# Gate and up products of two feed-forward layers: weights stationary, 256 token columns moving

## The chip, the core and the metric

The kernel runs on one core of one Trainium2 chip. The time is the device time of one execution in microseconds (us). Before the change three runs gave 2736.33, 2738.47 and 2739.03 us; their median is 2738.47. The profile is of one further execution.

## The reference

Two transformer blocks follow each other on 256 tokens of width 2048, all in float32. The first has a gated linear recurrence and sliding-window attention, the second gated linear attention; each ends in a SwiGLU feed-forward layer with a hidden width of 5632. Only these two layers are touched by the change:

```python
# first block: h2 is the normed x, scaled and shifted per channel
h2 = modulate(rms_norm(x, norm2_g[l]), sh2, sc2)
gate, up = jnp.split(h2 @ w_ffn_in[l], 2, axis=-1)
x = x + g2 * ((jax.nn.silu(gate) * up) @ w_ffn_out[l])
...
# second block
g, u = jnp.split(h @ w_gu, 2, axis=-1)
x = x + (jax.nn.silu(g) * u) @ w_down        # h = rms_norm(x) * gain
```

## The kernel before

Activations lie channel-major: 128 channels on the partitions, 256 tokens along the free axis. A group of 512 channels is one tile of 128x4x256 (a slot; there are 24).

**Weights.** Every weight matrix is streamed once, in chunks of 512 inputs x 512 outputs, 1 MB each. `split` loads a chunk into one of three `raw` buffers through SP's queue, and then works on halves (128x1024): ScalarE writes the rounded part `hi` (L173), VectorE the rest `lo` = raw - hi (L175). There are three `hi` and three `lo` buffers of half a chunk. A product of two numbers is made of three matmuls: hi x hi, hi x lo and lo x hi, so activations are kept as hi/lo pairs as well (`Pair`; `split_act` makes one, L225 and L226). A `tc.high_priority` block lets the scheduler put the loads and splits of weights ahead of other work.

**The two forms of `accumulate`.** In the plain form a block of 128x128 weights is the stationary operand and 256 token columns of the activation pair move (L197, L199, L201): 48 matmuls a chunk, whose result is channel-major. With `tokens=True` 128 tokens of the activation are stationary and 512 weight columns move (L190 to L192): 24 matmuls a chunk, whose result is token-major (128 tokens x 512 channels).

**The feed-forward layers.** `swiglu` is called twice, first with `gate1`, `up1`, `update1`, later with `gate2`, `up2`, `update2`. It takes the 11 groups of hidden channels in two parts, of 6 and of 5. For each group j `gate(j)` makes 4 chunks of the gate product (PSUM tiles `fgps`) and `up(sg, j)` 4 chunks of the up product (`fups`); then the down product (`fops`) runs over the groups of this part. So each layer has 88 chunks of gate and up and 44 of down.

Gate and up use `tokens=True`. What they leave in `sg` is token-major, but the down product needs channel-major. `turned` makes that: two `pump` steps after `up`, four 128x128 transposes on TensorE for each half group (L666, PSUM tile `tps`), then L668 and L669 write the hi and lo parts of `hid` straight from PSUM. A token's norm factor is then one number per partition; `by_token` (L336 on) turns the factor row into that column with two transposes. In layer 1's first group the norm's shift has to be added after the product, and it is a row of 512 (`fb`), which `matvec(..., row=True)` makes with one matmul that has ones as its stationary operand (L255).

**Order of work.** The kernel is plain Python that a scheduler orders per engine. `project` calls `pump` between chunks, which advances spawned generators (such as `second_norm`) and, by a credit, one step of a matrix-vector product (`ada_steps`: a load into one of five `mvw` buffers and one VectorE instruction, L247). In layer 1, two such strips of 16 steps run beside gate and up. `mvw` and `raw` loads share SP's queue there. Each engine runs its instructions in order.

Of the kernel before, what the change touches and what calls it, by code (L numbers as in the profile page):

```python
# [18 lines left out]
P = 128  # L19
# [30 lines left out]
def block_pair_kernel(ctx: ExitStack, tc: tile.TileContext, a: dict):  # L50
# [41 lines left out]
    def halves(t):  # L92
        return [t[:, 0:2, :], t[:, 2:4, :]]
# [85 lines left out]
    def accumulate(ps, ap, src, first, last, tokens=False):  # L179

        parts = split(ap, tokens)
        for kk in range(4):
            hi, lo = parts[kk // 2]
            wk = kk % 2
            fst, lst = first and kk == 0, last and kk == 3
            if tokens:
                for t in range(2):
                    tsl = slice(t * P, (t + 1) * P)
                    xh, xl = src.hi(kk)[:, tsl], src.lo(kk)[:, tsl]
                    nc.tensor.matmul(ps[t], xh, hi[:, wk, :], start=fst, stop=False)  # L190
                    nc.tensor.matmul(ps[t], xh, lo[:, wk, :], start=False, stop=False)  # L191
                    nc.tensor.matmul(ps[t], xl, hi[:, wk, :], start=False, stop=lst)  # L192
                continue
            for f in range(4):
                wsl = slice(f * P, (f + 1) * P)
                o = ps[f // 2][:, f % 2, :]
                nc.tensor.matmul(o, hi[:, wk, wsl], src.hi(kk), start=fst and f % 2 == 0,  # L197
                                 stop=False, skip_group_check=True)
                nc.tensor.matmul(o, hi[:, wk, wsl], src.lo(kk), start=False, stop=False,  # L199
                                 skip_group_check=True)  # L200
                nc.tensor.matmul(o, lo[:, wk, wsl], src.hi(kk), start=False, stop=lst,  # L201
                                 skip_group_check=True)

    def banks(name, tokens=False):
        return [bank(name, [P, 512] if tokens else [P, 2, T]) for _ in range(2)]
# [25 lines left out]
    nc.scalar.activation(cact, v("c", 0, 16), AF.Silu)  # L231
    mod = const.tile([P, 96], F32, name="mod")

    def matvec(srcs, col, width, done, queue=nc.gpsimd, row=False):


        state = {}

        def step(k):
            def run():  # L240
                w = mvw.tile([P, width], F32, tag="mvw", name="mvw")
                queue.dma_start(w, srcs[k])
                if k == 0:
                    state["acc"] = slot("mva", shape=[P, width])
                    nc.vector.tensor_scalar(state["acc"], w, col(0), None, ALU.mult)
                else:
                    nc.vector.scalar_tensor_tensor(state["acc"], w, col(k), state["acc"],  # L247
                                                   ALU.mult, ALU.add)
            return run

        def reduce():
            n = width // P
            ps = bank("mvp")
            if row:
                nc.tensor.matmul(ps[:, 0:width], ones, state["acc"], start=True, stop=True)  # L255
                done(ps[:, 0:width])
                return
            for f in range(n):
                nc.tensor.matmul(ps[:, f:f + 1], state["acc"][:, f * P:(f + 1) * P],
                                 ones[:, 0:1], start=True, stop=True)  # L260
            done(ps[:, 0:n])

        return [step(k) for k in range(NK)] + [reduce]
# [81 lines left out]
    def pair(ap):  # L345
        return ap.unsqueeze(1).to_broadcast([P, 2, T])
# [282 lines left out]
    while steps:  # L629
# [7 lines left out]
    steps += matvec([a["w_ffn_in"][0, k // 4][:, k % 4, :] for k in range(NK)],  # L637
                    lambda k: shift2[:, k:k + 1], 512, lambda ps: nc.vector.tensor_copy(fb, ps), nc.sync,
                    True)
    credit[0], credit[1] = 0.0, 1.3  # L640
    ssq = SumSq("ss2")
    gx = []
# [11 lines left out]
        steps.pop(0)()  # L654


    def turned(sv):

        p = Pair("hid")
        yield p  # L660
        for b in range(2):
            tp = bank("tps", [P, 2, T])
            for i in range(2):
                f = 2 * b + i
                for t in range(2):
                    nc.tensor.transpose(tp[:, i, t * P:(t + 1) * P], sv[:, t, f * P:(f + 1) * P],  # L666
                                        ident)
            nc.scalar.activation(p.his(b), tp, AF.Copy)  # L668
            nc.vector.tensor_tensor(p.los(b), tp, f32(p.his(b)), ALU.subtract)  # L669

    def swiglu(w_in, w_out, gate, up, update):
        for n, half in enumerate((range(0, 6), range(6, FG))):
            hid, turns = [], []
            for j in half:
                sg = gate(j)
                pump()
                gen = turned(up(sg, j))
                hid.append(next(gen))
                turns.append(spawn(gen, 2))
                pump()  # L680
            for f in range(NG):
                chunks = chunks_of(w_out, f, list(half))
                ps = banks("fops")
                for c in range(len(chunks)):
                    finish(turns[c])
                    accumulate(ps, chunks[c], hid[c], c == 0, c == len(chunks) - 1)
                    if c < len(chunks) - 1:
                        pump()
                update(n, f, ps)
                pump()  # L690

    h2 = [None] * NG
# [12 lines left out]
    norm_task = spawn(second_norm())  # L705

    def gate1(j):
        sg = slot("sg", shape=[P, 2, 512])
        ps = project(chunks_of("w_ffn_in", j), gx if j == 0 else h2, "fgps", True)
        if j == 0:  # L710
            finish(norm_task)
            for t in range(2):
                nc.vector.scalar_tensor_tensor(sg[:, t, :], ps[t], norm2["invp"][:, t:t + 1],
                                               fb, ALU.mult, ALU.add)
            nc.scalar.activation(sg, sg, AF.Silu)
        else:
            for t in range(2):
                nc.scalar.activation(sg[:, t, :], ps[t], AF.Silu)
        return sg

    def up1(sg, j):
        ps = project(chunks_of("w_ffn_in", FG + j), h2, "fups", True)
        for t in range(2):
            nc.vector.tensor_tensor(sg[:, t, :], ps[t], sg[:, t, :], ALU.mult)
        return sg

    steps += ada_steps(10, nc.sync) + ada_steps(11, nc.sync)
    credit[0], credit[1] = -6.0, 0.9
# [220 lines left out]
    norm5 = {}  # L949

    def last_norm():
        inv = inv_rms(ssq.mean(onesd), "inv5")
        yield 1
        norm5["inv"] = by_token(inv, "invp5")

    norm_task = spawn(last_norm(), 2)

    def gate2(j):
        sg = slot("sg", shape=[P, 2, 512])
        ps = project(chunks_of("ffn_w_gu", j), h2, "fgps", True)  # L960
        finish(norm_task)
        for t in range(2):
            nc.scalar.activation(sg[:, t, :], ps[t], AF.Silu, scale=norm5["inv"][:, t:t + 1])
        return sg

    def up2(sg, j):
        ps = project(chunks_of("ffn_w_gu", FG + j), h2, "fups", True)
        for t in range(2):
            nc.vector.scalar_tensor_tensor(sg[:, t, :], ps[t], norm5["inv"][:, t:t + 1],
                                           sg[:, t, :], ALU.mult, ALU.mult)  # L970
        return sg

    def update2(n, f, ps):
        for b, part in enumerate(halves(x[f])):
# [99 lines left out]
```

## Time and profile before

| | |
|---|---|
| median of three runs | 2738.47 us (2736.33 to 2739.03) |
| the profiled execution, its own time | 2733.5 us |
| span of that execution | 2731.7 us |
| granted TensorE clock | 0.999 |
| 512-column matmuls of gate and up | 4224 (L190 to L192, three groups each of `fgps` and `fups`) |
| first matmul of layer 1's gate to layer 1's end | about 856 to 1589 us |
| layer 2 | from about 1998 us to the end |

How to read the quoted lines. A page of the profile gives, by engine, busy time, share of the span and number of instructions. A row of groups gives line, engine, operation, out<-in by the program's names, shapes, count, busy time, the mean ns of one, and the idle time before it with what ended it. A row of waits gives who waited for whom, the total in us, how often, and the longest. A row of the timeline gives start (us), length (us), engine, line and operation, with a count where equal ones are merged, and in brackets the idle time before. A matmul's length contains its passage through the array, so the pace is read from the distance between starts.

### The profile page before, as it was taken

The numbers are of one execution on the slowest core, as the hardware profiler recorded it, in microseconds if no ns is written. First come the engines' busy times: TensorE is split into PE (matmuls) and PEld (weight loads), VectorE is DVE, ScalarE is ACT, GpSimd is POOL, SyncE is SP. The second block draws the span as 40 slices with busy tenths as digits, with TensorE's granted clock in tenths as the row PEclk, the third lists the DMA queues.
The fourth block names the chain that finished last, engine by engine and source line by source line (L and its number), as shares of the span: only waits on it lengthen the run. The fifth ranks groups of instructions, "written<-read, shape, count | busy, mean of one in ns | idle before, by whom it ended". The sixth has DMA issues, their size and how long they took to land.

```text
span 2731.7 us, 43911 instructions
## 1 busy us (share of the span) xinstructions
PE 2680.5 (98%) x18612; PEld 2479.3 (91%) x18612; DVE 1782.3 (65%) x2000; ACT 1310.7 (48%) x1525; POOL 25.7 (1%) x52
## 2 busy tenths in 40 slices
PE   4999999999999999999999999999999999999999
PEld 3999999999999888999888999899988889988899
DVE  8887876888887865444545667866654544444544
ACT  3446637864445444434444545655544444344443
POOL 1100000000000000000000000000000000000000
PEclk9999999999999999999999999999999999999999
DMA  9984696769875866555555544444555555555554
GB/s 351 370 311 147 221 341 226 273 243 351 336 278 194 311 238 217 186 200 187 191 192 185 195 170 170 142 152 171 200 186 187 195 188 188 199 186 194 190 195 161
DMA packets 100166, 602.00 MB, mean 220 GB/s; under 512 B 11121, under 2 KB 11633, under 8 KB 40577
## 3 DMA queue, kind: packets, MB, share of 16 engines
q1 hardware_dynamic: 93056, 574.03, 59.1%
q0 software_dynamic: 6912, 25.17, 2.3%
q8 instruction: 145, 2.38, 0.3%
q14 instruction: 53, 0.43, 0.0%
HBM read 597.06 MB, written 2.10 MB: 219 GB/s over the span
## 4 chain that ended last, share of the span: by engine, by line
PE 95%; DVE 2%; issue 1%; DMA 1%; ACT 1%; SPq 0%; DVEq 0%; ACTq 0%
PE fgps L192 6%; PE fgps L191 6%; PE fgps L190 6%; PE fops L197 6%; PE fups L190 6%; PE fups L192 6%; PE fups L191 6%; PE fops L201 6%; PE fops L199 6%; PE part L197 2%; PE part L199 2%; PE part L201 2%; PE lops L201 1%; PE ups L197 1%; PE wops L197 1%; PE ups L201 1%
## 5 line engine op out<-in xcount | busy, mean ns | idle before, releaser
L175 DVE TENSOR_TENSOR lo<-raw,hi 128x1024 fp32r<-128x1024 f32 x928 | 1134.3, 1224 | 842.9 <-ACT hi L173 841.2
L173 ACT ACTIVATE hi<-raw 128x1024 fp32r<-128x1024 f32 x928 | 983.1, 1060 | 1270.4 <-PE fups L192 274.5
L197 PE MATMUL fops<-hid,hi 128*128 128x256 f32 x1408 | 389.0, 276 | 0.0
L201 PE MATMUL fops<-hid,lo 128*128 128x256 f32 x1408 | 388.7, 276 | 0.0
L199 PE MATMUL fops<-hid,hi 128*128 128x256 f32 x1408 | 388.6, 276 | 0.0
L190 PE MATMUL fups<-hi,h 128*128 128x512 f32 x704 | 274.0, 389 | 0.0
L192 PE MATMUL fups<-hi,h 128*128 128x512 f32 x704 | 273.9, 389 | 0.0
L191 PE MATMUL fups<-lo,h 128*128 128x512 f32 x704 | 273.9, 389 | 0.0
L199 PEld LDWEIGHTS fops<-hid,hi 128*128 128x128 f32 x1408 | 264.3, 188 | 0.1
L197 PEld LDWEIGHTS fops<-hid,hi 128*128 128x128 f32 x1408 | 264.3, 188 | 0.2
L201 PEld LDWEIGHTS fops<-hid,lo 128*128 128x128 f32 x1408 | 264.3, 188 | 0.0
L190 PE MATMUL fgps<-hi,h 128*128 128x512 f32 x672 | 263.5, 392 | 0.0
L192 PE MATMUL fgps<-hi,h 128*128 128x512 f32 x672 | 261.8, 390 | 0.0
L191 PE MATMUL fgps<-lo,h 128*128 128x512 f32 x672 | 261.6, 389 | 0.0
L247 DVE SCALAR_TENSOR_TENSOR mva<-mvw,cact,mva 128x1024 f32<-128x1024 f32 x180 | 230.6, 1281 | 26.6 <-DMA mvw<-ada_w 24.5
L191 PEld LDWEIGHTS fups<-lo,h 128*128 128x128 f32 x704 | 132.2, 188 | 27.4
L190 PEld LDWEIGHTS fups<-hi,h 128*128 128x128 f32 x704 | 132.2, 188 | 27.4
L192 PEld LDWEIGHTS fups<-hi,h 128*128 128x128 f32 x704 | 132.2, 188 | 27.4
L192 PEld LDWEIGHTS fgps<-hi,h 128*128 128x128 f32 x672 | 126.1, 188 | 26.2
L190 PEld LDWEIGHTS fgps<-hi,h 128*128 128x128 f32 x672 | 126.2, 188 | 25.6
L191 PEld LDWEIGHTS fgps<-lo,h 128*128 128x128 f32 x672 | 126.2, 188 | 25.5
L197 PE MATMUL part<-h,hi 128*128 128x256 f32 x512 | 145.2, 284 | 0.0
(322 smaller groups left out, 5410.7 us busy)
## 6 DMA issues: line engine op xcount, KB each, us to landing
raw<-w_in SPq DMA_DIRECT2D x88, 1024.0 KB, 5.7
raw<-w_ffn_in SPq DMA_DIRECT2D x88, 1024.0 KB, 4.9
raw<-ffn_w_gu SPq DMA_DIRECT2D x88, 1024.0 KB, 4.8
mvw<-ada_w SPq DMA_DIRECT2D x144, 512.0 KB, 7.0
raw<-gla_w_in SPq DMA_DIRECT2D x48, 1024.0 KB, 4.9
raw<-w_ffn_out SPq DMA_DIRECT2D x44, 1024.0 KB, 4.8
raw<-ffn_w_down SPq DMA_DIRECT2D x44, 1024.0 KB, 4.9
mvw<-ada_w POOLq DMA_DIRECT2D x48, 512.0 KB, 8.5
```

The costliest lines, as they stand in the source:

```text
L173: nc.scalar.activation(hi, rb, AF.Copy)
L175: nc.vector.tensor_tensor(lo, rb, f32(hi), ALU.subtract)
L190: nc.tensor.matmul(ps[t], xh, hi[:, wk, :], start=fst, stop=False)
L191: nc.tensor.matmul(ps[t], xh, lo[:, wk, :], start=False, stop=False)
L192: nc.tensor.matmul(ps[t], xl, hi[:, wk, :], start=False, stop=lst)
L197: nc.tensor.matmul(o, hi[:, wk, wsl], src.hi(kk), start=fst and f % 2 == 0, stop=False, skip_group_check=True)
L199: nc.tensor.matmul(o, hi[:, wk, wsl], src.lo(kk), start=False, stop=False, skip_group_check=True)
L201: nc.tensor.matmul(o, lo[:, wk, wsl], src.hi(kk), start=False, stop=lst, skip_group_check=True)
L247: nc.vector.scalar_tensor_tensor(state["acc"], w, col(k), state["acc"], ALU.mult, ALU.add)
```

## The change

Gate and up now use the plain form, as the rest of the kernel does. Their result is channel-major, so `turned` goes, and `split_act` makes `hid` right behind the product. The norm factor multiplies as a row broadcast over partitions (`pair(inv)`), so both `by_token` calls of these layers go. In layer 1's first group VectorE multiplies by the factor and ScalarE adds the shift as a bias, from an `fb` of 128x4. In layer 2 ScalarE could take the factor as a scale before; now VectorE multiplies the gate product by it, ScalarE takes Silu of the whole group into a new tile `sv`, and VectorE multiplies that by the factor again, which stands for the factor on the up product.

```diff
-    fb = slot("fb", shape=[P, 512])
+    fb = slot("fb", shape=[P, 4])
...
-                gen = turned(up(sg, j))
-                hid.append(next(gen))
-                turns.append(spawn(gen, 2))
+                hid.append(up(sg, j))
                 pump()
             for f in range(NG):
-                chunks = chunks_of(w_out, f, list(half))
...
-                    finish(turns[c])
-                    accumulate(ps, chunks[c], hid[c], c == 0, c == len(chunks) - 1)
...
+                update(n, f, project(chunks_of(w_out, f, list(half)), hid, "fops"))
...
-        norm2["invp"] = by_token(norm2["inv"], "invp2")
...
     def gate1(j):
-        sg = slot("sg", shape=[P, 2, 512])
-        ps = project(chunks_of("w_ffn_in", j), gx if j == 0 else h2, "fgps", True)
+        sg = slot("sg")
+        ps = project(chunks_of("w_ffn_in", j), gx if j == 0 else h2, "fgps")
         if j == 0:
             finish(norm_task)
-            for t in range(2):
-                nc.vector.scalar_tensor_tensor(sg[:, t, :], ps[t], norm2["invp"][:, t:t + 1],
-                                               fb, ALU.mult, ALU.add)
-            nc.scalar.activation(sg, sg, AF.Silu)
+            for b, part in enumerate(halves(sg)):
+                nc.vector.tensor_tensor(part, ps[b], pair(norm2["inv"]), ALU.mult)
+            for f in range(4):
+                nc.scalar.activation(sg[:, f, :], sg[:, f, :], AF.Silu, bias=fb[:, f:f + 1])
...
     def up1(sg, j):
-        ps = project(chunks_of("w_ffn_in", FG + j), h2, "fups", True)
-        for t in range(2):
-            nc.vector.tensor_tensor(sg[:, t, :], ps[t], sg[:, t, :], ALU.mult)
-        return sg
+        ps = project(chunks_of("w_ffn_in", FG + j), h2, "fups")
+        for b, part in enumerate(halves(sg)):
+            nc.vector.tensor_tensor(part, ps[b], part, ALU.mult)
+        return split_act(sg, "hid")
...
     def gate2(j):
-        sg = slot("sg", shape=[P, 2, 512])
-        ps = project(chunks_of("ffn_w_gu", j), h2, "fgps", True)
+        sg = slot("sg")
+        ps = project(chunks_of("ffn_w_gu", j), h2, "fgps")
         finish(norm_task)
-        for t in range(2):
-            nc.scalar.activation(sg[:, t, :], ps[t], AF.Silu, scale=norm5["inv"][:, t:t + 1])
-        return sg
+        for b, part in enumerate(halves(sg)):
+            nc.vector.tensor_tensor(part, ps[b], norm5["inv"], ALU.mult)
+        sv = slot("sv")
+        nc.scalar.activation(sv, sg, AF.Silu)
+        for b, part in enumerate(halves(sv)):
+            nc.vector.tensor_tensor(part, part, norm5["inv"], ALU.mult)
+        return sv
 
     def up2(sg, j):
-        ps = project(chunks_of("ffn_w_gu", FG + j), h2, "fups", True)
-        for t in range(2):
-            nc.vector.scalar_tensor_tensor(sg[:, t, :], ps[t], norm5["inv"][:, t:t + 1],
-                                           sg[:, t, :], ALU.mult, ALU.mult)
-        return sg
+        ps = project(chunks_of("ffn_w_gu", FG + j), h2, "fups")
+        for b, part in enumerate(halves(sg)):
+            nc.vector.tensor_tensor(part, ps[b], part, ALU.mult)
+        return split_act(sg, "hid")
```

Up to the end of the `w_o` product every engine's instructions stand as before. Behind it the scheduler orders anew; three places matter.

TensorE in layer 1 before, in the second group's gate product, where the first group's transposes stand:

```order
L191 MATMUL fgps<-lo,h 128x512
L192 MATMUL fgps<-hi,h 128x512
L666 MATMUL tps<-ident,sg 128x128 x8
L190 MATMUL fgps<-hi,h 128x512
L191 MATMUL fgps<-lo,h 128x512
```

TensorE now, where the first group's up product ends and the second group's gate product begins:

```order
L197 MATMUL fups<-h,hi 128x256
L199 MATMUL fups<-h,hi 128x256
L201 MATMUL fups<-h,lo 128x256
L197 MATMUL fgps<-h,hi 128x256
L199 MATMUL fgps<-h,hi 128x256
L201 MATMUL fgps<-h,lo 128x256
```

No transpose stands between products any more, and a chunk has 48 rows of 256 columns in place of 24 of 512.

VectorE in layer 2 before, over one group (`lo` is the weights' split, the others belong to the group):

```order
L669 TENSOR_TENSOR hid<-tps,hid 128x2x256 x2
L175 TENSOR_TENSOR lo<-raw,hi 128x1024 x13
L969 SCALAR_TENSOR_TENSOR sg<-fups,invp_20063,sg 128x512 x2
L175 TENSOR_TENSOR lo<-raw,hi 128x1024 x3
L669 TENSOR_TENSOR hid<-tps,hid 128x2x256 x2
```

VectorE in layer 2 now, over one group; L932 waits for the gate product's last matmul, L936 for ScalarE's Silu, L942 for the up product's last matmul, L226 (in `split_act`) for ScalarE's hi part:

```order
L932 TENSOR_TENSOR sg<-fgps,inv_22077 128x512 x2
L175 TENSOR_TENSOR lo<-raw,hi 128x1024
L936 TENSOR_TENSOR sv<-sv,inv_22077 128x512 x2
L175 TENSOR_TENSOR lo<-raw,hi 128x1024 x7
L942 TENSOR_TENSOR sv<-fups,sv 128x512 x2
L175 TENSOR_TENSOR lo<-raw,hi 128x1024
L226 TENSOR_TENSOR hid<-sv,hid 128x2x256 x2
L175 TENSOR_TENSOR lo<-raw,hi 128x1024 x7
```

Four instructions for each group have become eight, and at each product's end they stand ahead of the first and of the second `lo` that follow.

VectorE in layer 1 before, from the first group's up product on (`mva` are the steps of the matrix-vector strip):

```order
L247 SCALAR_TENSOR_TENSOR mva<-mvw,cact,mva 128x1024
L175 TENSOR_TENSOR lo<-raw,hi 128x1024
L724 TENSOR_TENSOR sg<-fups,sg 128x512
L175 TENSOR_TENSOR lo<-raw,hi 128x1024
L724 TENSOR_TENSOR sg<-fups,sg 128x512
L247 SCALAR_TENSOR_TENSOR mva<-mvw,cact,mva 128x1024
```

VectorE in layer 1 now, from the same point:

```order
L694 TENSOR_TENSOR sg<-fups,sg 128x512 x2
L175 TENSOR_TENSOR lo<-raw,hi 128x1024
L226 TENSOR_TENSOR hid<-sg,hid 128x2x256 x2
L244 TENSOR_SCALAR mva<-mvw,cact 128x1024
L175 TENSOR_TENSOR lo<-raw,hi 128x1024
L246 SCALAR_TENSOR_TENSOR mva<-mvw,cact,mva 128x1024 x2
L175 TENSOR_TENSOR lo<-raw,hi 128x1024
L246 SCALAR_TENSOR_TENSOR mva<-mvw,cact,mva 128x1024
L175 TENSOR_TENSOR lo<-raw,hi 128x1024
L246 SCALAR_TENSOR_TENSOR mva<-mvw,cact,mva 128x1024 x2
```

The strip's first step stood ahead of the up product's end and now stands behind the first group's `hid`. On SP's queue the loads are the same in number; one more `raw` load is put ahead of the strip's `mvw` loads that wait for those steps.

More of the change, by code (lines that the diff above doesn't have):

```diff
@@ L232, in block_pair_kernel, with matvec @@
     mod = const.tile([P, 96], F32, name="mod")
-    def matvec(srcs, col, width, done, queue=nc.gpsimd, row=False):
+    def matvec(srcs, col, width, done, queue=nc.gpsimd):
         state = {}
@@ L253, in reduce @@
             ps = bank("mvp")
[L254 to L257, printed above, removed]
             for f in range(n):
@@ L654, in block_pair_kernel @@
         steps.pop(0)()
[L657 to L664, printed above, removed]
-                for t in range(2):
[L666 to L669, printed above, removed]
     def swiglu(w_in, w_out, gate, up, update):
         for n, half in enumerate((range(0, 6), range(6, FG))):
-            hid, turns = [], []
+            hid = []
             for j in half:
@@ L676, in swiglu @@
                 pump()
-                gen = turned(up(sg, j))
-                hid.append(next(gen))
-                turns.append(spawn(gen, 2))
+                hid.append(up(sg, j))
                 pump()
             for f in range(NG):
-                chunks = chunks_of(w_out, f, list(half))
-                ps = banks("fops")
-                for c in range(len(chunks)):
-                    finish(turns[c])
-                    accumulate(ps, chunks[c], hid[c], c == 0, c == len(chunks) - 1)
-                    if c < len(chunks) - 1:
-                        pump()
-                update(n, f, ps)
+                update(n, f, project(chunks_of(w_out, f, list(half)), hid, "fops"))
                 pump()
@@ L707, in gate1 @@
     def gate1(j):
-        sg = slot("sg", shape=[P, 2, 512])
-        ps = project(chunks_of("w_ffn_in", j), gx if j == 0 else h2, "fgps", True)
+        sg = slot("sg")
+        ps = project(chunks_of("w_ffn_in", j), gx if j == 0 else h2, "fgps")
         if j == 0:
             finish(norm_task)
-            for t in range(2):
-                nc.vector.scalar_tensor_tensor(sg[:, t, :], ps[t], norm2["invp"][:, t:t + 1],
-                                               fb, ALU.mult, ALU.add)
-            nc.scalar.activation(sg, sg, AF.Silu)
-        else:
-            for t in range(2):
-                nc.scalar.activation(sg[:, t, :], ps[t], AF.Silu)
+            for b, part in enumerate(halves(sg)):
+                nc.vector.tensor_tensor(part, ps[b], pair(norm2["inv"]), ALU.mult)
+            for f in range(4):
+                nc.scalar.activation(sg[:, f, :], sg[:, f, :], AF.Silu, bias=fb[:, f:f + 1])
+        else:
+            for b, part in enumerate(halves(sg)):
+                nc.scalar.activation(part, ps[b], AF.Silu)
         return sg
     def up1(sg, j):
-        ps = project(chunks_of("w_ffn_in", FG + j), h2, "fups", True)
-        for t in range(2):
-            nc.vector.tensor_tensor(sg[:, t, :], ps[t], sg[:, t, :], ALU.mult)
-        return sg
+        ps = project(chunks_of("w_ffn_in", FG + j), h2, "fups")
+        for b, part in enumerate(halves(sg)):
+            nc.vector.tensor_tensor(part, ps[b], part, ALU.mult)
+        return split_act(sg, "hid")
     steps += ada_steps(10, nc.sync) + ada_steps(11, nc.sync)
@@ L951, in last_norm @@
     def last_norm():
-        inv = inv_rms(ssq.mean(onesd), "inv5")
+        norm5["inv"] = pair(inv_rms(ssq.mean(onesd), "inv5"))
         yield 1
-        norm5["inv"] = by_token(inv, "invp5")
     norm_task = spawn(last_norm(), 2)
     def gate2(j):
-        sg = slot("sg", shape=[P, 2, 512])
-        ps = project(chunks_of("ffn_w_gu", j), h2, "fgps", True)
+        sg = slot("sg")
+        ps = project(chunks_of("ffn_w_gu", j), h2, "fgps")
         finish(norm_task)
-        for t in range(2):
-            nc.scalar.activation(sg[:, t, :], ps[t], AF.Silu, scale=norm5["inv"][:, t:t + 1])
-        return sg
-    def up2(sg, j):
-        ps = project(chunks_of("ffn_w_gu", FG + j), h2, "fups", True)
-        for t in range(2):
-            nc.vector.scalar_tensor_tensor(sg[:, t, :], ps[t], norm5["inv"][:, t:t + 1],
-                                           sg[:, t, :], ALU.mult, ALU.mult)
-        return sg
+        for b, part in enumerate(halves(sg)):
[5 more added lines that the diff above has]
+        return sv
+    def up2(sg, j):
+        ps = project(chunks_of("ffn_w_gu", FG + j), h2, "fups")
+        for b, part in enumerate(halves(sg)):
+            nc.vector.tensor_tensor(part, ps[b], part, ALU.mult)
+        return split_act(sg, "hid")
     def update2(n, f, ps):
```

3 lines of the change are left out of this document (1 added, 2 removed).

## The prediction

> **What bounds the kernel now.** I read the busy table first, then TensorE's own waits, then everybody's waits.
>
> ```profile
> PE 2680.5 (98%) x18612; PEld 2479.3 (91%) x18612; DVE 1782.3 (65%) x2000; ACT 1310.7 (48%) x1525; POOL 25.7 (1%) x52
> PE mvp L259 <- DVE mva L247: 38.1, 3, 35.0
> ...
> PE gkps L201 <- DVE lo L175: 2.3, 3, 0.9
> ...
> DVE lo L175 <- ACT hi L173: 841.2, 627, 5.6
> ACT hi L173 <- PE fups L192: 274.5, 173, 3.5
> ```
>
> TensorE is busy 98% of the span, and a busy TensorE could still be slow, so the waits matter more. TensorE's waits are listed by tile: the largest is 38.1 us before the first product, and no row names `fgps`, `fups` or `fops`. In the feed-forward layers TensorE never waits; the others do. ScalarE waits for the up product's matmuls to free a `hi` buffer (274.5 us, 173 times), VectorE waits for ScalarE. The weight stream is ahead and is held back by TensorE. So every TensorE slot in these layers is on the path, and the question is what the change does to those slots.
>
> **The pace of both forms.** The timeline of TensorE gives starts. First the 512-column form, then the 256-column form in the down product of the same layer; the rows are 24 and 48 matmuls apart, one chunk each.
>
> ```profile
> 895.05 0.39 PE L192 MATMUL fups<-hi,h 128*128 128x512 f32 x1
> ...
> 900.49 0.39 PE L192 MATMUL fups<-hi,h 128*128 128x512 f32 x1
> 1180.03 0.28 PE L201 MATMUL fops<-hid,lo 128*128 128x256 f32 x1
> ...
> 1185.47 0.28 PE L201 MATMUL fops<-hid,lo 128*128 128x256 f32 x1
> ```
>
> Both chunks take 5.44 us: 24 x 226.7 ns and 48 x 113.3 ns. Twice as many matmuls and weight loads of the array, half the columns, the same time. So the 176 chunks of gate and up should cost nothing either way. Each chunk can be misread by 0.02 us (two starts rounded to 0.01), which is 176 x 0.02 = 3.5 us on the sum.
>
> The Trainium skill says otherwise (TensorE: Matmul & The Clock Gate, section "Wait — 56ns, not 53.3ns?"): a warm matmul costs its columns at 2.4 GHz and a fixed 2.5 ns. By it the 4224 extra matmuls would cost 4224 x 2.5 ns = 10.6 us, an estimate from that page. The rows above speak against that here: two 256-column matmuls show 226.7 ns, as one of 512 does. It is weighed below as a rival, from a row.
>
> **What the change removes.** A group's transposes, in layer 2, with ScalarE's `hi` rows around them, which follow TensorE's releases:
>
> ```profile
> 2090.62 1.06 ACT L173 ACTIVATE hi<-raw 128x1024 fp32r<-128x1024 f32 x1 [1.66 <-PE fgps L192]
> 2093.34 1.06 ACT L173 ACTIVATE hi<-raw 128x1024 fp32r<-128x1024 f32 x1 [1.66 <-PE fgps L192]
> 2094.31 1.07 ACT L668 ACTIVATE hid<-tps 128x512 fp32r<-128x512 f32 x2
> 2096.97 1.06 ACT L173 ACTIVATE hi<-raw 128x1024 fp32r<-128x1024 f32 x1 [1.59 <-PE fgps L192]
> 2093.14 1.03 PE L666 MATMUL tps<-ident,sg 128*128 128x128 f32 x8
> 2093.93 0.48 PE L190 MATMUL fgps<-hi,h 128*128 128x512 f32 x1
> L666 PE MATMUL tps<-ident,sg 128*128 128x128 f32 x176 | 22.8, 272 | 0.0
> ```
>
> Half a chunk takes 2.72 us (2093.34 - 2090.62), the half with the transposes 3.63 (2096.97 - 2093.34). The block of 8 costs 0.91 us: 0.79 until the next product's matmul (2093.93 - 2093.14), the rest in the first matmul behind it, 0.48 long in place of 0.39. The 176 transposes are 22 blocks: **22 x 0.91 = 20.0 us**, all of it on the path.
>
> Both `by_token` calls go, four transposes. Two of them:
>
> ```profile
> 872.86 0.39 PE L192 MATMUL fgps<-hi,gx 128*128 128x512 f32 x1
> 873.10 0.27 PE L341 MATMUL tokps<-ident,inv 128*128 128x128 f32 x1
> ...
> 874.38 0.40 PE L191 MATMUL fgps<-lo,gx 128*128 128x512 f32 x1
> ```
>
> From 872.86 to 874.38 lie five product matmuls, 5 x 0.227 = 1.13 us, and 0.39 more. I take as much for the other pair at most, 0 at least, so **0.4 to 0.8 us, 0.6**.
>
> The row product for `fb` becomes four single-column matmuls:
>
> ```profile
> 843.96 0.28 PE L201 MATMUL wops<-m,lo 128*128 128x256 f32 x1
> 844.08 1.02 PE L255 MATMUL mvp<-mva,ones 128*128 128x512 f32 x2
> ...
> 845.05 0.28 PE L199 MATMUL wops<-m,hi 128*128 128x256 f32 x1
> 1001.36 1.84 PE L259 MATMUL mvp<-ones,mva 128*128 128x1 f32 x16
> 1003.06 0.49 PE L190 MATMUL fgps<-hi,h 128*128 128x512 f32 x1
> ```
>
> It costs 845.05 - 843.96 - 2 x 0.113 = 0.86 us now. Eight such columns cost 1.70 (1003.06 - 1001.36), so four about 0.85, between 0 and 1.7: **0, within 0.9 either way**.
>
> **What it adds, and what hides it.** A half's buffer comes free when TensorE ends the half three before. TensorE needs it two halves later, 5.44 us. The undisturbed stretch in layer 2:
>
> ```profile
> 2085.18 1.06 ACT L173 ACTIVATE hi<-raw 128x1024 fp32r<-128x1024 f32 x1 [1.66 <-PE fups L192]
> 2086.27 1.23 DVE L175 TENSOR_TENSOR lo<-raw,hi 128x1024 fp32r<-128x1024 f32 x1 [1.49 <-ACT hi L173]
> 2087.41 1.40 DVE L969 SCALAR_TENSOR_TENSOR sg<-fups,invp,sg 128x512 f32<-128x512 f32 x2
> L724 DVE TENSOR_TENSOR sg<-fups,sg 128x512 f32<-128x512 f32 x22 | 14.2, 683 | 0.0
> L226 DVE TENSOR_TENSOR yr<-ge,yr 128x512 fp32r<-128x512 f32 x8 | 5.1, 685 | 0.0
> L225 ACT ACTIVATE yr<-ge 128x512 fp32r<-128x512 f32 x8 | 4.6, 621 | 5.1 <-DVE ge L603 5.1
> L927 ACT ACTIVATE sr<-sr 128x1024 f32<-128x1024 f32 x4 | 4.2, 1052 | 0.0
> ```
>
> `hi` starts at 2085.18, `lo` ends at 2087.50, 2.3 us later: 3.1 us are spare. Now the wait that layer 2 adds: VectorE's L932 waits for the gate product's last matmul, and behind it stand the weights' `lo`. Count from that end as 0. L932 twice, 2 x 0.68, ends at 1.4; the next `lo` at 2.6, due at 5.4. Silu of the group (1.05, as L927) runs on ScalarE behind a `hi` from 1.4 to 2.5, so L936 need not wait at 2.6 and ends at 4.0. The second `lo` has its `hi` at 2.72 + 1.06 = 3.8, ends at 5.2 and is due at 8.16. The up product's end goes alike: L942 1.4, `lo` 2.6, ScalarE's two L225 (2 x 0.62) by 2.7, L226 4.0, `lo` 5.2. Nearly 3 us stay spare, so **0**. VectorE gets 2.7 us more a group (eight of 0.68 for four of 0.70), 30 us over 11 groups; it has them:
>
> ```profile
> core 0: us, PE busy (x) PEld busy (x) DVE busy (x) ACT busy (x) POOL busy (x), PEclk, DMA share, GB/s
> 855.00:1126.00 271.00, 271.00 (x1237) 225.20 (x1236) 186.01 (x198) 125.38 (x141) 0.00 (x0) 1.00 0.67 239
> 2020.00:2265.00 245.00, 245.00 (x1103) 203.32 (x1102) 121.54 (x109) 106.94 (x112) 0.00 (x0) 1.00 0.55 189
> ```
>
> It is busy 121.5 of 245 us in the first part of layer 2. Layer 1 is tighter, 186 of 271, because of the strips.
>
> ```profile
> 912.21 2.60 DVE L247 SCALAR_TENSOR_TENSOR mva<-mvw,cact,mva 128x1024 f32<-128x1024 f32 x2
> 914.72 1.22 DVE L175 TENSOR_TENSOR lo<-raw,hi 128x1024 fp32r<-128x1024 f32 x1
> 915.86 1.28 DVE L247 SCALAR_TENSOR_TENSOR mva<-mvw,cact,mva 128x1024 f32<-128x1024 f32 x1
> 917.05 1.22 DVE L175 TENSOR_TENSOR lo<-raw,hi 128x1024 fp32r<-128x1024 f32 x1
> SPq L152 <- DVE lo L175: 2289.0, 450, 15.1
> ```
>
> Back to back a step takes 1.2 us and a `lo` 1.14 (starts of these rows). Walked in the new order from the first up product's end, `hid` and the late strip included, each `lo` still ends ahead of its due time, by 1.2 us at the least (the fourth behind that end: 15.1 against 16.3). So 0 again, but with the thinnest cover of all. SP's `raw` loads wait for `lo` (2289 us in all), hence a `raw` load put ahead of `mvw` loads loses nothing; behind an `mvw` load that waits for a step, it waits for a step that VectorE runs before the `lo` it needs anyway. The last groups' `hid` is first read four chunks into the down product, 21 us later, so nothing is late at the turn, and the tail of the program is the same.
>
> **Sum.** 20.0 + 0.6 + 0 + 0 = 20.6 us off the profiled execution's 2733.5 (span 2731.7), so 2712.9 there. The median of the runs is 5 us above that execution; I subtract from the median: 2738.5 - 20.6 = **2718**. Its own range is 2714 to 2722 (3.5 us for the pace, 0.9 for `fb`).
>
> **Rivals.**
>
> (a) *Each extra matmul costs something.* A 256-column stage that is less smooth:
>
> ```profile
> L197 PE MATMUL wops<-m,hi x256: 276/276/682, 767.8 to 855.5; 128*128 128x256 f32 x128
> ```
>
> 255 steps of three matmuls in 87.7 us are 1.0 above 255 x 0.340; were that the form and not the `fb` product inside it (0.86), it would be 0.063 us a chunk, 176 x 0.063 = 11 us: 2718 + 11 = **2729**. The down product's 5.44 speaks against it. The skill's fixed 2.5 ns, named above, would end at 2718 + 10.6, nearly the same. Chance 0.10.
>
> (b) *VectorE comes late with `lo`, slower.* At 44 ends of products VectorE stands in line ahead of the split. In the `gkps` stage it already made TensorE wait, 2.3 us in 3 times, 0.77 each. At all 44 ends that is 34 us: 2718 + 34 = **2752**. It decides when each end loses over 20.6 / 44 = 0.47 us, that is, when `lo` comes 3.5 us later than worked out. For it: one queue in order, more work at each end. Against: the spare 3 us. Chance 0.04 in full, 0.06 for a part, between 2722 and 2738, in layer 1 above all.
>
> (c) *The weights become the bound,* and TensorE waits for them where the transposes stood: **2738**. Against it, ScalarE sits idle 1.66 us of each 2.72 until TensorE releases a buffer. Chance 0.03.
>
> (d) *The change does not do what it says.* The order has no L666 row left. What could remain is a slow pass somewhere else: 0.02, anywhere.
>
> **How the numbers follow.** The forecast has 0.75. I hold 0.8 and more between 2714 and 2730: forecast, (a), and half of (b)'s part. About 0.2%, 5.5 us, can be told from no change here. Faster: 0.75 + 0.10 + 0.06 + half of (d), rounded 0.92. Same: (c) and what touches it, 0.04. Slower: (b) in full, 0.04.
>
> **What the profile will show.** Right: no L666; starts of `fgps` and `fups` 5.44 us a chunk apart; TensorE's waits still without `fgps`, `fups`, `fops`; the layers 20 us shorter, 0.91 a group. Wrong: a row "PE fups <- DVE lo" (b), chunks of 5.50 us (a), or waits for `raw` (c).

## The result and the profile after

| | before | after |
|---|---|---|
| median of the runs timed beside each other | 2738.75 us (2736.33 to 2740.61, 4 runs) | 2714.46 us (2712.07 to 2719.20, 4 runs) |
| the profiled execution | 2733.5 us, span 2731.7 | 2713.72 us, span 2712.0 |
| granted TensorE clock | 0.999 | 0.999 |

The ratio is 0.9921, with a 95% interval from 0.9909 to 0.9934: about 21.6 us less (0.0079 x 2738.75), between 18 and 25. The two medians are 24.3 us apart, which is inside that interval.

The busy table, TensorE's waits and the two large waits of the others, as shown of before, now of the profile after:

```profile
PE 2660.3 (98%) x22662; PEld 2625.8 (97%) x22662; DVE 1805.1 (67%) x2040; ACT 1310.1 (48%) x1517; POOL 25.7 (1%) x52
PE mvp L254 <- DVE mva L246: 36.6, 2, 35.0
...
PE gkps L201 <- DVE lo L175: 2.3, 3, 0.9
...
DVE lo L175 <- ACT hi L173: 787.8, 612, 5.5
ACT hi L173 <- PE fups L199: 266.2, 170, 3.5
```

TensorE has 4050 more instructions (22662 for 18612) and is busy 20.2 us less; its share stays 98%. No row of the view names `fgps`, `fups` or `fops`, as before. VectorE is busy 23 us more and waits less for ScalarE: it had the time. The share of the weight loads (PEld) went from 91% to 97%, which comes back below.

TensorE's timeline after, rows 48 matmuls apart:

```profile
2069.75 0.28 PE L201 MATMUL fups<-h,lo 128*128 128x256 f32 x1
...
2075.19 0.28 PE L201 MATMUL fups<-h,lo 128*128 128x256 f32 x1
...
2080.63 0.28 PE L201 MATMUL fgps<-h,lo 128*128 128x256 f32 x1
```

A chunk takes 5.44 us, the last one across the turn from the up product to the next gate product too.

Where did the time go? The starts that bound the stages, from TensorE's timeline before and then after: the first matmul of layer 1, the first behind it, the first of layer 2, the last of the kernel.

```profile
855.83 0.40 PE L190 MATMUL fgps<-hi,gx 128*128 128x512 f32 x1
1588.95 0.28 PE L197 MATMUL gkps<-h,hi 128*128 128x256 f32 x1
1998.55 0.40 PE L190 MATMUL fgps<-hi,h 128*128 128x512 f32 x1
2727.72 0.28 PE L201 MATMUL fops<-hid,lo 128*128 128x256 f32 x1
```

```profile
856.75 0.28 PE L197 MATMUL fgps<-gx,hi 128*128 128x256 f32 x1
1579.41 0.28 PE L197 MATMUL gkps<-h,hi 128*128 128x256 f32 x1
1989.05 0.28 PE L197 MATMUL fgps<-h,hi 128*128 128x256 f32 x1
2707.93 0.28 PE L201 MATMUL fops<-hid,lo 128*128 128x256 f32 x1
```

Their differences, and the same rows of every later run:

| kernel | ahead of layer 1 | layer 1 | between | layer 2 |
|---|---|---|---|---|
| before | 855.83 | 733.12 | 409.60 | 729.17 |
| after | 856.75 | 722.66 | 409.64 | 718.88 |
| after, `a0_same_chip` | 855.13 | 724.80 | 409.62 | 718.88 |
| after, `a1_once_more` | 857.18 | 726.67 | 409.61 | 718.88 |
| `e1_wide_no_turns` | 860.79 | 723.18 | 409.64 | 719.24 |
| `e2_narrow_with_turns` | 863.16 | 732.84 | 409.63 | 728.71 |
| `e3_lump_256` | 855.53 | 723.94 | 409.60 | 718.88 |
| `e3_lump_512` | 859.47 | 723.68 | 409.59 | 718.88 |
| `e3_lump_1024` | 857.02 | 723.14 | 409.63 | 798.06 |
| `e4_up2_128_columns` | 856.83 | 722.66 | 409.62 | 951.35 |
| `e5_strip_own_queue` | 855.63 | 723.35 | 409.59 | 718.89 |
| `e6_strip_earlier` | 862.10 | 724.99 | 409.60 | 718.88 |

Layer 1 is 10.46 us shorter and layer 2 10.29, together 20.75; what lies between is the same to 0.04 us. Two things are to be read from the table before the experiments. The stretch ahead of layer 1, whose instructions the change leaves as they were but for the `fb` product, moves by 8 us from execution to execution (855 to 863): most of the scatter of the whole times is there, and its cause stays open. So the stages are the finer measure, and layer 2 of the changed kernel repeats (718.88 to 718.89 us). And layer 1 of the same changed kernel took 722.66, 724.80 and 726.67 us, which the prediction has no term for.

### The profile page after: what moved, and what is told of

Read it like the earlier page. It is cut to its first block, busy times and chain, and to the rows that moved or that the text cites. A ratio compares the mean times of both kernels' runs of the same rounds, so it can differ in the third digit from the quotient of the medians.

```text
span 2712.0 us, 52234 instructions
## 1 busy us (share of the span) xinstructions
PE 2660.3 (98%) x22662; PEld 2625.8 (97%) x22662; DVE 1805.1 (67%) x2040; ACT 1310.1 (48%) x1517; POOL 25.7 (1%) x52
## 4 chain that ended last, share of the span: by engine, by line
PE 93%; DVE 3%; DMA 2%; issue 1%; ACT 1%; SPq 0%; DVEq 0%; ACTq 0%
PE fgps L201 6%; PE fups L201 6%; PE fgps L197 6%; PE fops L197 6%; PE fups L197 6%; PE fups L199 6%; PE fgps L199 6%; PE fops L201 6%; PE fops L199 6%; PE part L197 2%; PE part L199 2%; PE part L201 2%; DMA mvw<-ada_w 2%; DVE mva L246 1%; PE wops L201 1%; PE grps L199 1%
## 5 line engine op out<-in xcount | busy, mean ns | idle before, releaser
L197 PE MATMUL fups<-h,hi 128*128 128x256 f32 x1408 | 388.7, 276 | 0.0
L199 PE MATMUL fups<-h,hi 128*128 128x256 f32 x1408 | 388.6, 276 | 0.0
L201 PE MATMUL fups<-h,lo 128*128 128x256 f32 x1408 | 388.6, 276 | 0.0
L197 PE MATMUL fgps<-h,hi 128*128 128x256 f32 x1344 | 371.3, 276 | 0.0
L201 PE MATMUL fgps<-h,lo 128*128 128x256 f32 x1344 | 371.0, 276 | 0.0
L199 PE MATMUL fgps<-h,hi 128*128 128x256 f32 x1344 | 371.0, 276 | 0.0
L199 PEld LDWEIGHTS fups<-h,hi 128*128 128x128 f32 x1408 | 264.3, 188 | 0.0
L197 PEld LDWEIGHTS fups<-h,hi 128*128 128x128 f32 x1408 | 264.3, 188 | 0.0
L201 PEld LDWEIGHTS fups<-h,lo 128*128 128x128 f32 x1408 | 264.3, 188 | 0.0
L199 PEld LDWEIGHTS fgps<-h,hi 128*128 128x128 f32 x1344 | 252.3, 188 | 0.0
L197 PEld LDWEIGHTS fgps<-h,hi 128*128 128x128 f32 x1344 | 252.3, 188 | 0.0
L201 PEld LDWEIGHTS fgps<-h,lo 128*128 128x128 f32 x1344 | 252.3, 188 | 0.0
```

## The experiments

**The changed kernel beside the others.** No edit.

> The changed kernel again, beside the others. My theory: 20.6 us below the kernel before (ratio 0.9925), span about 2711 to 2712. If a fixed cost for each extra matmul were real, 10 to 11 us below (0.996).

Measured: 2714.22 us, ratio 0.9915 (0.9900 to 0.9930). The gain is there again. The row that the prediction named as a sign against it, TensorE waiting for `lo` in `fups`, is there once:

```profile
932.32 0.28 PE L199 MATMUL fups<-h,hi 128*128 128x256 f32 x1
934.42 0.39 PE L201 MATMUL fups<-h,lo 128*128 128x256 f32 x1 [1.82 <-DVE lo L175]
```

The next two rows are VectorE's at that time:

```profile
931.95 1.28 DVE L246 SCALAR_TENSOR_TENSOR mva<-mvw,cact,mva 128x1024 f32<-128x1024 f32 x1 [4.23 <-DMA mvw<-ada_w]
933.15 1.22 DVE L175 TENSOR_TENSOR lo<-raw,hi 128x1024 fp32r<-128x1024 f32 x1
```

VectorE had nothing else to do for 4.23 us, but its queue is in order: a step of the strip waited for its own `mvw` load, and the `lo` that TensorE needed stood behind it.

**Only the transposes out, the 512-column form kept.**

```diff
-    def turned(sv):
+    def as_is(sv):
         p = Pair("hid")
-        yield p
         for b in range(2):
-            tp = bank("tps", [P, 2, T])
-            ...
-            nc.scalar.activation(p.his(b), tp, AF.Copy)
-            nc.vector.tensor_tensor(p.los(b), tp, f32(p.his(b)), ALU.subtract)
+            part = sv[:, b, :].rearrange("p (a t) -> p a t", t=T)
+            nc.scalar.activation(p.his(b), part, AF.Copy)
+            nc.vector.tensor_tensor(p.los(b), part, f32(p.his(b)), ALU.subtract)
+        return p
...
-                gen = turned(up(sg, j))
-                hid.append(next(gen))
-                turns.append(spawn(gen, 2))
+                hid.append(as_is(up(sg, j)))
```

> The kernel before, 512 columns moving, without its transposes: the token-major products are split and used as if channel-major, so the hidden values are not the reference's. My theory (the transposes are the whole gain, the two forms keep the same pace): 20.0 us below the kernel before, 0.6 us above the changed kernel; ratio 0.9927. Rival, the form itself gains or costs: if each extra matmul costs 2.5 ns, this one is 10 us faster than the changed kernel; if the 256-column form is faster, it stays up to 20 us behind it.

Measured: 2716.15 us, ratio 0.9921 (0.9908 to 0.9933); layer 1 723.18 and layer 2 719.24 us. Without any change of the form, 9.94 and 9.93 us of the 10.46 and 10.29 are gone. 0.52 and 0.36 us are left to the changed kernel. This kernel still has one `by_token` call in each layer, and TensorE's timeline shows what they cost; each pair of rows is five product matmuls and two transposes apart:

```profile
877.83 0.39 PE L192 MATMUL fgps<-hi,gx 128*128 128x512 f32 x1
...
879.34 0.39 PE L191 MATMUL fgps<-lo,gx 128*128 128x512 f32 x1
2010.64 0.39 PE L192 MATMUL fgps<-hi,h 128*128 128x512 f32 x1
...
2012.02 0.40 PE L191 MATMUL fgps<-lo,h 128*128 128x512 f32 x1
```

Less 5 x 0.227 us, that is 0.38 and 0.25 us. So 0.14 and 0.11 us a layer remain for the form of 88 chunks and everything else. If that is the form, the one with more matmuls is the faster by a thousandth of a microsecond or two a chunk, which is next to nothing. The `fb` product is not in these layers: it stands inside `wops`, ahead of layer 1, in every kernel. In the profile after:

```profile
844.93 0.95 PE L254 MATMUL mvp<-ones,mva 128*128 128x1 f32 x8
845.94 0.28 PE L199 MATMUL wops<-m,hi 128*128 128x256 f32 x1
```

One product matmul lies between as well, so the eight cost 1.01 - 0.11 = 0.90 us, for 0.86 before.

**The changed form, and the transposes put back.** The tile that a group's up product leaves is transposed eight times, two `pump` steps behind that product and so beside the next group's gate product, and nobody reads the result.

```diff
+    last = [None]
+
+    def idle_turns(sv):
+        yield 2
+        for b in range(2):
+            tp = bank("tps", [P, 2, T])
+            for i in range(2):
+                for t in range(2):
+                    nc.tensor.transpose(tp[:, i, t * P:(t + 1) * P],
+                                        sv[:, 2 * b + i, t * P:(t + 1) * P], ident)
...
                 hid.append(up(sg, j))
+                turn = idle_turns(last[0])
+                next(turn)
+                turns.append(spawn(turn, 2))
...
+        last[0] = sg
```

> The changed kernel with eight 128x128 transposes for each group put back, where they stood before, their results unread. My theory: 22 x 0.91 = 20.0 us above the changed kernel, 0.6 us below the kernel before (ratio 0.9998). Rival, TensorE had slack beside the transposes, or the gain came from elsewhere (the hidden values made earlier, fewer waits): nothing or clearly less than 15 us comes back.

Measured: 2734.59 us, ratio 0.9993 (0.9983 to 1.0003), no difference from before; layer 1 is 10.18 and layer 2 9.83 us longer than after. A block in TensorE's timeline of this run:

```profile
2055.40 0.28 PE L201 MATMUL fgps<-h,lo 128*128 128x256 f32 x1
2055.51 1.04 PE L659 MATMUL tps<-ident,sv 128*128 128x128 f32 x8
2056.31 0.36 PE L197 MATMUL fgps<-h,hi 128*128 128x256 f32 x1
2056.51 0.28 PE L199 MATMUL fgps<-h,hi 128*128 128x256 f32 x1
```

From 2055.40 to 2056.51 lie two product matmuls, 2 x 0.113 us, and eight transposes, which take the other 0.88 us. Here nothing waits for them and they wait for nothing, and still they cost their whole time: 20.0 us in both layers (10.18 + 9.83) for 22 blocks, 0.91 each on the average.

**How much cover layer 2 has.** The changed kernel with one more VectorE instruction, a reciprocal whose result is not read, at each of the 22 product ends of layer 2, ahead of the instructions that take the gate or up product out of PSUM; 256, 512 or 1024 columns wide, which took 1.75, 3.35 and 6.55 us. The first two read the first of the product's two PSUM tiles, `ps[0]`. The large one reads `sg` behind these instructions instead. The middle one's edit in the gate product; the up product has the same:

```diff
+        with tc.high_priority(offset=2 * PREP):
+            nc.vector.reciprocal(spare.rearrange("p (a t) -> p a t", t=T), ps[0])
             for b, part in enumerate(halves(sg)):
                 nc.vector.tensor_tensor(part, ps[b], norm5["inv"], ALU.mult)
```

> The changed kernel with one extra VectorE instruction (reciprocal of 256 PSUM columns into a tile nobody reads, about 1.75 us as inv5 took) ahead of the evacuation at each of the 22 ends of gate and up products of the second layer. My theory of the cover: the next lo ends at 1.75 + 1.3 + 1.23 = 4.3 us, due at 5.4: span unchanged (within 1 us). Rival, the cover is thinner than worked out: up to 22 x 1.75 = 38 us more.

> The same with 512 columns, about 3.45 us. My theory: lo ends at 3.45 + 1.3 + 1.23 = 6.0 us, due at 5.4 (5.7 for the first matmul that reads it): 0.3 to 0.6 us at each of 22 ends, 7 to 13 us more, with a row of TensorE waiting for lo. Rivals: nothing, if buffers give more cover than that; or 22 x 3.45 = 76 us, if there is none.

> The same with 1024 elements read from the evacuated tile, about 6.9 us, behind the evacuation. My theory: lo ends at 1.3 + 6.9 + 1.23 = 9.4 us, 3.7 to 4.0 late at each of 22 ends: 81 to 88 us more. Rivals: nothing; or 22 x 6.9 = 152 us.

Measured, one execution each: 2713.74, 2717.43 and 2793.66 us. Layer 2 took 718.88 us with the small and with the middle one, the same as with none, and 798.06 with the large one. The middle one was expected to show and does not; that its whole time is higher comes from ahead of layer 1 (2.72 us against after) and from layer 1 (1.02), not from the edit.

First the cover with no lump: behind a gate product's end of the profile after, the `lo` on VectorE and the first matmul that reads it.

```profile
2056.43 1.23 DVE L175 TENSOR_TENSOR lo<-raw,hi 128x1024 fp32r<-128x1024 f32 x1 [0.29 <-ACT hi L173]
2060.91 0.28 PE L201 MATMUL fups<-h,lo 128*128 128x256 f32 x1
```

The `lo` ends 3.2 us early, and so it does at the other ends; the least in layer 2 is 1.9, once, at the layer's start. VectorE and then ScalarE around an up product's end of `e3_lump_512`:

```profile
2080.30 3.35 DVE L946 RECIPROCAL spare<-fups 128x512 f32<-128x512 f32 x1
2083.57 1.22 DVE L948 TENSOR_TENSOR sv<-fups,sv 128x512 f32<-128x512 f32 x2
2084.71 2.35 DVE L175 TENSOR_TENSOR lo<-raw,hi 128x1024 fp32r<-128x1024 f32 x2
2080.78 1.06 ACT L173 ACTIVATE hi<-raw 128x1024 fp32r<-128x1024 f32 x1 [1.66 <-PE fups L199]
```

The `lo` of the `hi` that starts at 2080.78 runs from 2084.71 to some 2085.9, 5.1 us behind the start of that `hi`, in place of 2.3 where nothing stands in the way. The first matmul that reads it starts on time:

```profile
2086.36 0.28 PE L201 MATMUL fgps<-h,lo 128*128 128x256 f32 x1
```

That leaves 0.4 us, and about as much at every end. The product itself ended 50 matmuls ahead of this row, 5.67 us, at 2080.69. So the due time of the theory (5.4 to 5.7 behind the product's end) was right, and its 6.0 us for the end of `lo` was too long: the lump starts at 2080.30, 0.4 us ahead of the product's end, since `ps[0]` is done before the second tile, and the instructions follow one another faster than their lengths add up. `lo` ended 5.2 us behind the product's end.

ScalarE, VectorE and TensorE of `e3_lump_1024`, a gate product's end:

```profile
2012.56 1.06 ACT L173 ACTIVATE hi<-raw 128x1024 fp32r<-128x1024 f32 x1 [1.66 <-PE fgps L199]
2013.40 6.55 DVE L936 RECIPROCAL spare<-sg 128x1024 f32<-128x1024 f32 x1
2019.87 3.43 DVE L175 TENSOR_TENSOR lo<-raw,hi 128x1024 fp32r<-128x1024 f32 x3
2018.25 0.28 PE L199 MATMUL fups<-h,hi 128*128 128x256 f32 x1
2021.08 0.39 PE L201 MATMUL fups<-h,lo 128*128 128x256 f32 x1 [2.56 <-DVE lo L175]
```

At the pace of 0.113 us the matmul behind 2018.25 was due at 2018.36, 5.8 us behind the start of that `hi`, and came 2.72 us late; the 2.56 of the wait count from the modelled end of the matmul before. (The scheduler put two `hi` matmuls more ahead of this one at each of the 22 ends, which is why 5.8 stands here and 5.6 in the middle case.) TensorE's waits of this run have 2.56 us at every one of the 22 ends:

```profile
PE fups L201 <- DVE lo L175: 28.1, 11, 2.6
PE fgps L201 <- DVE lo L175: 23.0, 9, 2.6
PE fops L201 <- DVE lo L175: 5.1, 2, 2.6
```

That makes 56.2 us, and the layer is 79.18 longer. The rest is a second effect. Two windows of 8 us, each from the restart behind such a wait; the columns are busy time by engine with the number of instructions, then the granted clock, the share of the DMA engines and GB/s:

```profile
2071.94:2079.94 8.00, 8.00 (x55) 8.00 (x56) 4.67 (x6) 2.12 (x2) 0.00 (x0) 0.79 0.55 163
2047.31:2055.31 8.00, 8.00 (x70) 8.00 (x71) 5.86 (x6) 2.19 (x3) 0.00 (x0) 1.00 0.66 213
```

Behind one wait TensorE started 70 matmuls in 8 us, behind another 55, at a granted clock of 0.79. The same window behind each of the 22 waits shows 0.79 ten times and 1.00 twelve times. From a restart with the full clock to the next restart lay 24.63 us, 2.87 more than four chunks (21.76): the 2.72 and 0.15 in the first matmuls behind the wait. From one with the lowered clock it was 26.23, another 1.6. 22 x 2.87 + 10 x 1.6 = 79.1, the whole of it. The sum came out near what was expected (81 to 88) by luck: the delay was smaller than expected, and a clock that no theory had named made up for it.

**What a matmul costs at the least.** The changed kernel with layer 2's up product in pieces of 128 columns, 96 matmuls a chunk.

```diff
+                for m in range(0, T, wide):
+                    cs = slice(m, m + wide)
+                    o = ps[f // 2][:, f % 2, cs]
+                    nc.tensor.matmul(o, hi[:, wk, wsl], src.hi(kk)[:, cs],
+                                     start=fst and f % 2 == 0 and m == 0,
+                                     stop=False, skip_group_check=True)
...
-        ps = project(chunks_of("ffn_w_gu", FG + j), h2, "fups")
+        ps = project(chunks_of("ffn_w_gu", FG + j), h2, "fups", wide=P)
```

> The changed kernel with the up product of the second layer in 128 columns a matmul: 96 matmuls for a chunk in place of 48, 44 chunks. If time goes with the columns alone: no change. With a fixed 2.5 ns for a matmul: 44 x 48 x 2.5 ns = 5 us more. My theory: below some width the load of the stationary block sets the pace; eight 128-column transposes took 0.91 us, 0.114 each, so a chunk takes up to 96 x 0.114 = 10.9 us in place of 5.44 and the kernel up to 240 us more, and 256 columns are near the narrowest that is free.

Measured: 2946.26 us in one execution, layer 2 232.47 us longer. TensorE's timeline, two starts that are 96 matmuls apart:

```profile
2039.77 0.27 PE L204 MATMUL fups<-h,lo 128*128 128x128 f32 x1
...
2050.49 0.27 PE L204 MATMUL fups<-h,lo 128*128 128x128 f32 x1
```

10.72 us, 0.1117 a matmul: half the columns, and the same pace as with 256 (0.1133). The 44 chunks cost 44 x 5.28 = 232 more. So halving the columns from 512 to 256 costs nothing, and halving them once more, to 128, nearly doubles a chunk's time. Where between 128 and 256 columns that begins was not measured.

**Why layer 1 differs from execution to execution.** Three kernels on one chip: the changed one once more, then two edits.

> The changed kernel once more, unchanged, beside the next two. In one earlier execution of it TensorE waited 1.8 us in layer 1 for a lo that stood behind a strip step (mva) waiting 4.23 us for its own mvw load; in another it did not wait. Theory (the step's load comes late by chance): layer 1 is between 722.7 and 725 us again, layer 2 718.9, time 2712 to 2718. Rival (the order of the queue decides): the same length as in one of the two to 0.1 us.

Measured: 2716.40 us, ratio 0.9932 (0.9919 to 0.9944), layer 1 726.67 us, longer than either theory said. Its timeline, VectorE and then TensorE:

```profile
934.23 1.28 DVE L246 SCALAR_TENSOR_TENSOR mva<-mvw,cact,mva 128x1024 f32<-128x1024 f32 x1 [4.67 <-DMA mvw<-ada_w]
936.70 0.39 PE L201 MATMUL fups<-h,lo 128*128 128x256 f32 x1 [2.05 <-DVE lo L175]
938.24 0.42 PE L201 MATMUL fups<-h,lo 128*128 128x256 f32 x1
941.63 0.28 PE L197 MATMUL fups<-h,hi 128*128 128x256 f32 x1
```

The two windows behind the restart, with the columns of the windows above:

```profile
936.00:940.00 4.00, 3.30 (x21) 3.30 (x22) 4.00 (x4) 0.00 (x0) 0.00 (x0) 0.77 0.64 244
940.00:945.00 5.00, 5.00 (x39) 5.00 (x39) 3.84 (x5) 2.12 (x2) 0.00 (x0) 0.84 0.95 323
```

The step waited 4.67 us for its load and TensorE 2.05 for the `lo` behind the step. Then the granted clock fell to 0.77 and 0.84: from 938.24 to 941.63, 3.39 us, lie 16 matmuls, 0.212 each in place of 0.113, which is 1.6 us lost. The wait with its restart and the clock make nearly all of the 4.0 us against the first execution. In the first profile after, the same step waited less:

```profile
930.77 1.28 DVE L246 SCALAR_TENSOR_TENSOR mva<-mvw,cact,mva 128x1024 f32<-128x1024 f32 x1 [2.50 <-DMA mvw<-ada_w]
```

2.50 us, and TensorE did not wait. The three `e3_lump` kernels and `e4_up2_128_columns` have layer 1 in the same order on VectorE and on SP's queue, so there are seven executions of it, and the same step waits in all:

| | the step's wait for its load | TensorE's wait behind it | layer 1 |
|---|---|---|---|
| after | 2.50 | none | 722.66 |
| `e4_up2_128_columns` | 2.54 | none | 722.66 |
| `e3_lump_1024` | 3.06 | none | 723.14 |
| `e3_lump_256` | 3.61 | 0.98 | 723.94 |
| `e3_lump_512` | 3.88 | 0.71 | 723.68 |
| `a0_same_chip` | 4.23 | 1.82 | 724.80 |
| `a1_once_more` | 4.67 | 2.05 | 726.67 |

Where TensorE waited, the step's wait is 2.4 to 3.2 us longer than TensorE's, and that is the cover at this place. So the rival falls: with one order, layer 1 has six different lengths. Even where TensorE did not wait, in the first profile after, the cover was nearly used up at another place, behind a step that waited 3.13 us; VectorE, and the first matmul that reads this `lo`:

```profile
1032.16 1.22 DVE L175 TENSOR_TENSOR lo<-raw,hi 128x1024 fp32r<-128x1024 f32 x1
1033.81 0.28 PE L201 MATMUL fgps<-h,lo 128*128 128x256 f32 x1
```

The `lo` ended at 1033.38, 0.43 us early.

The first edit puts the strips' loads on GpSimd's queue:

```diff
-    steps += ada_steps(10, nc.sync) + ada_steps(11, nc.sync)
+    steps += ada_steps(10) + ada_steps(11)
```

> The changed kernel with layer 1's 32 mvw loads issued from GpSimd's queue in place of SP's, where they stand behind raw loads that wait for a free buffer. Theory (a strip step that waits for its own load, in VectorE's queue ahead of a lo, is what breaches the cover): no mva waits over 2 us, no row of TensorE waiting for lo in fgps or fups, layer 1 at 722.7 us; the whole time 0 to 2 us less, which is under what a ratio can tell. Rival (strips and lo are too much for VectorE here, whatever the loads): a wait of TensorE for lo stays, layer 1 724 or more.

Measured: 2715.73 us, ratio 0.9930 (0.9915 to 0.9945); layer 1 723.35 us, layer 2 as after. The longest wait of a step for its load is 0.40 us, as the theory has it, and one wait of TensorE is left, as the rival has it:

```profile
936.21 0.39 PE L201 MATMUL fups<-h,lo 128*128 128x256 f32 x1 [0.39 <-DVE lo L175]
```

Both are right in part. The late load was most of it. But the scheduler ordered VectorE anew in this kernel, with three strip steps more ahead of this `lo`, and in that order VectorE's own work is a little more than fits.

The second edit begins the strips earlier and spreads them more:

```diff
-    credit[0], credit[1] = -6.0, 0.9
+    credit[0], credit[1] = -3.0, 0.8
```

> The changed kernel with layer 1's strips begun three credits earlier and at 0.8 step a chunk in place of 0.9, loads on SP's queue as before. Theory of the late load: the loads keep their place behind raw loads, so a breach of 0 to 2 us may stay; layer 1 722.7 to 725 us. Rival (too many steps in a row): spread further, no step stands in the way any more, layer 1 at 722.7 us and no wait for lo.

Measured: 2716.45 us, ratio 0.9935 (0.9921 to 0.9948); layer 1 724.99 us. A step waited 3.33 us for its load and TensorE 1.16 us for a `lo`; in one further place it was 3.98 and 0.31. In this execution spreading the steps did not help while the loads stand behind `raw` loads; the rival falls. Neither edit can be told from the changed kernel in the whole time (0.9930 and 0.9935 beside 0.9932). Layer 1 of both kernels was profiled once.

## Why the prediction was right, point by point

- **TensorE is on the path everywhere in the two layers: right.** Eight transposes that nothing waits for cost 0.91 us a block in `e2_narrow_with_turns`, and taken out alone they give nearly the whole gain in `e1_wide_no_turns`. No row of TensorE's waits names `fgps`, `fups` or `fops` in the profile after, so rival (b) in full and rival (c) fall.
- **Both forms have the same pace, 5.44 us a chunk: right.** The chunk measures 5.44, and between `e1_wide_no_turns` and after, less `by_token`, lie 0.14 and 0.11 us in layers of 88 chunks, with the form of more matmuls the shorter one. Rival (a) falls: at 0.063 us a chunk each layer would have been 5.5 us longer than in that run. So does the fixed 2.5 ns a matmul of the Trainium skill (TensorE: Matmul & The Clock Gate, section "Wait — 56ns, not 53.3ns?"): 2112 more matmuls in each layer would be 5.3 us, an estimate from that page, and they are not there. That both forms are equal was seen, not understood: `e4_up2_128_columns` shows that with 128 columns it no longer holds, which the prediction did not ask.
- **The transposes, 20.0 us: right.** 9.94 + 9.93 by taking them out, 10.18 + 9.83 by putting them back.
- **`by_token` 0.6 and `fb` 0: right.** The rows of `e1_wide_no_turns` give 0.38 + 0.25 = 0.63 us for the two `by_token` calls. `fb` became eight single-column matmuls, not four, since each of its four columns stands as two in the profile; at 0.90 us for 0.86 the term stays near 0.
- **Layer 2's waits are hidden: right.** The prediction had nearly 3 us spare; 3.2 are measured at the products' ends, 1.9 at the least. Lumps of 1.75 and 3.35 us do not show, and one of 6.55 makes TensorE 2.72 us late.
- **Layer 1's waits are hidden: wrong in some executions.** The step that failed is the walk of VectorE's queue in the new order, "each `lo` still ends ahead of its due time, by 1.2 us at the least". It gave each strip step its own time and let it start at once. The runs show a step that waits 2.50 to 4.67 us for its `mvw` load, with a `lo` behind it, at a place where 2.4 to 3.2 us are to spare. In seven executions TensorE waited in four, and layer 1 took 0 to 4.0 us more than in the first profile. That this profile came out as forecast there was luck: its least cover was 0.43 us, not 1.2. It is rival (b)'s mechanism, in layer 1 as that rival said, but once in a layer and not at the products' ends. The sentence on the `mvw` load looked at whether `raw` loads come late behind it, and not at whether the load itself does.
- **Sum.** 20.6 us were worked out and the stages give 20.75: 19.87 for the transposes, 0.63 for `by_token`, and 0.25 that no term has. The profiled execution was to take 2712.9 us and took 2713.7, since layer 1 began 0.9 us later. Against the median, 2718 was forecast; the ratio puts it at 2717 (0.9921 x 2738.75), the median of four runs at 2714.46.

## What to carry over

A transpose on an engine that never waits costs all of its time, so to drop it for a form with more and shorter matmuls pays as long as the shorter ones keep the pace. That is read from the starts of both forms in the trace; a run with one size below shows how near the limit is. Where work is added to an engine with an in-order queue, walk that queue with the instructions' own waits in it: an instruction that waits for its DMA holds up all behind it, whatever room the engine's busy time shows. A pause of two or three microseconds of TensorE may cost more than itself, when the clock falls behind it.

## What was unexpected of the hardware

**A floor under a matmul.** 128 moving columns with a weight load for each took 0.1117 us, 256 took 0.1133, 512 took 0.2267. The strip's 16 single-column matmuls, which multiply plain float32 values, took 1.70 us (1001.36 to 1003.06 in the profile before), 0.106 each, so the floor hardly depends on the columns. With 256 columns the weight loads are busy 97% of the span. Whether it is the load that sets the floor was not tested.

**The clock falls behind short pauses.** Behind waits of 2.05 and 2.56 us TensorE ran some 3.4 us at 0.212 us a 256-column matmul, about half pace, and lost 1.6 us, though not every time: 10 of 22 times at 2.56 us, not behind this wait's shorter forms (1.82 us and less in layer 1). The trace's record of the granted clock says which times. In `e3_lump_1024` the ten stretches at half clock in layer 2 last 3.41 us each, and from the first, at 2021.83, they begin at whole multiples of 3.413 us (15, 15, 22, 15, 60, 8, 22, 15 and 15 from one to the next). Cut time into such windows: the ten pauses before a fall have 1.94 us or more of their 2.56 in one window, and the fall begins with the next; the other twelve lie across two, with 1.85 at the most in either. The pause of 2.05 us in `a1_once_more` has 1.95 in one window, that of 1.82 in `a0_same_chip` 1.19. So in these streams of matmuls the limit lay between 1.85 and 1.94 us of pause in one window. The Trainium skill (TensorE: Matmul & The Clock Gate, section "What's actually happening") has half the clock after at least one idle window of about 3.4 us, and a window that runs freely. The half pace and the length of 3.4 us agree with these rows, and so does a result that depends on where the pause falls; that the pause must be as long as the window does not.
